# A hybrid decoder layer on one core: small products of a pair of heads gathered into fewer groups on TensorE

## The chip, the core and the metric

The kernel runs on one core of a Trainium2 chip. The metric is the device time of one execution in microseconds (us). A core has TensorE (matrix products, written PE in the profile), VectorE (DVE), ScalarE (ACT), GpSimd (POOL) and SyncE (SP, which here issues the transfers). Products write into PSUM, which is divided into banks; a bank here holds a tile of 128 x 512 in fp32.

## The reference, cut to what matters

One layer with width 2048 and 512 tokens. A single input projection feeds two token mixers; their outputs are projected up, merged by gates, projected out, and a per-layer embedding and two norms follow.

```
h = rmsnorm(x);  z = h @ w_in          # columns: r,k,v,g (RWKV), q,k,v,g (FoX), gates
# RWKV-7, 16 heads of 64, one step per token:
s_kk = S @ kk_t
S = S * w_t - outer(s_kk, kk_t * a_t) + outer(v_t, k_t);   y_t = S @ r_t
y = group_norm(y) + (sum r*k*r_k) * v;   y_rw = y * silu(g)
# FoX, 16 heads of 64, causal blocks of 128 queries:
logits = q k^T / 8 + (c_q - c_k);  probs = softmax(causal(logits));  o = probs @ v
y_fox = o * silu(g)
merged = sigmoid(gate_rw) * (y_rw @ w_up_rwkv) + sigmoid(gate_fox) * (y_fox @ w_up_fox)
x = x + merged @ w_out
x = x + (p @ ple_proj) * sigmoid(rmsnorm(x) @ ple_gate_w);   out = rmsnorm(x)
```

## The kernel before, in words

**Weight products.** Activations lie transposed, a tile being 128 columns of the width by all 512 tokens. Each fp32 weight is split into a high part (`hi`, a cast on ScalarE, L154) and a rest (`lo`, a subtraction on VectorE, L155), and so are the activations (`xh`, `xl`). Per tile of 128 rows of a weight three products of 128 x 512 are summed: xh with hi, xl with hi, xh with lo. `main` (L788) is a generator that issues them step by step: for each of eight pairs of heads p the eight projections rw_k, rw_v, rw_r, rw_g, fx_k, fx_q, fx_v, fx_g (128 columns each, 48 products each), then gates (`gate`), upward projections (`up`), output (`wo`) and embedding (`pp`, `pg`).

**Small products.** What the two mixers compute is small fp32 work. `rw_mixer` (L413) and `fox_mixer` (L685) are coroutines, one of each per pair. `Tensor` (L54) adds up an estimated time of TensorE, in ns; `Streams` (L73) resumes a coroutine when the number of ns that its last `yield` named have passed. It then issues a few products, which so stand between the weight products. TensorE's order is thus set by the yields. The other engines' order, and with it that of their waits, is set by a scheduler that looks at readiness in its own estimate; only the `keep` operations hold their places. An engine works its queue strictly in order.

**RWKV of a pair.** Tokens go in eight chunks of 64, q = 0, 1 being halves of four chunks. After transposing the inputs (`at`, `bt`, `kt`, L484 to L503), the products of a chunk give the matrices inside it (`gb`, L526; `gk`, L541). A part of gb, `lt`, goes through HBM and comes back spread over partitions as `lr` (L537 to L540). With it VectorE inverts 32 x 32 triangles by 60 operations in a row on `tp` and `nn` (L571 to L579). The inverses leave by transfer into `mdr` and come back twice, as `mt` and as the diagonal blocks; both land in the buffer `bd`. Two transposes on VectorE (L588) make from it the `x` that the products x3 and x4 (L590 to L602) combine; x3's result is copied by ScalarE at L595. Then `u` (L606), `tr` and `py` (L618 to L634), the state chunk by chunk (`st`, L636 to L643), group norm with a power on GpSimd (L656 to L667), and the output.

**Attention of a pair.** Two heads, four blocks of 128 queries each. Per block: decays (GpSimd, L721); logits `lg` on TensorE; a reduction on VectorE that masks and takes the maximum (`nm`, L732); exponential (ScalarE, L734), reciprocal (VectorE, L735), scaling (ScalarE, L736); transposes `pT` on TensorE (L755); a copy `pt` (ScalarE, L758); values `po` on TensorE (L769). Once per pair the values are transposed too (`fvt`, L689, copied at L693).

**Banks.** main has two banks for weight products, "A" two (gb, gk, u, x, transposes of RWKV), "F" one (lg, pT, fvt), "Y" two (py), "O" one (po). A group that needs a bank waits until its last reader is through. `pt` has two buffers.

**Names.** A name in the order has the pair behind it (x3 of pair 6 is x36); attention's have head and block (pT12_0: head 12, block 0), and a number that only tells one use of a buffer from another.

Of the kernel before, what the change touches and what calls it, by code (L numbers as in the profile page):

```python
# [15 lines left out]
F32 = mybir.dt.float32  # L16
# [7 lines left out]
P = 128  # L24
T = 512
# [82 lines left out]
def build(tc, a, out, dbg=None):  # L108
# [3 lines left out]
    v, s, g, dma = nc.vector, nc.scalar, nc.gpsimd, nc.sync  # L112
    keep = tc.keep_in_program_order
    pe = Tensor(nc.tensor)
# [118 lines left out]
    for h in range(2):  # L233
        hs = slice(64 * h, 64 * h + 64)
# [44 lines left out]
    psx = mix.enter_context(tc.tile_pool(name="psx", bufs=1, space=PSUM))  # L279
# [11 lines left out]
    small = {}  # L291
# [105 lines left out]
    def b2(name):  # L397
        return big.tile([P, T], F32, tag="b2", bufs=B2, name=name)

    def b4(shape, name):  # L400
        return big.tile(shape, F32, tag="b4", bufs=7, name=name)

    def psa(shape, name):
        return psx.tile(shape, F32, tag="A", bufs=2, name=name)

    def c3(t):
        return t.rearrange("p (c t) -> p c t", t=64)

    def need(z, *names):
        while any(n not in z for n in names):  # L410
            yield 450

    def rw_mixer(p, z):  # L413
# [12 lines left out]
        for h in range(2):  # L426
            cs = slice(P * h, P * h + P)
            v.tensor_tensor(lul[half(h), cs], lur[half(h), cs], luh[half(h), cs].bitcast(F32), op=ALU.subtract)
        yield 4700
        for h, (dst, hc) in enumerate(((sig, p), (aa, 8 + p))):  # L430
            cs = slice(P * h, P * h + P)
            ps = psa([P, T], f"lo{h}_{p}")
# [19 lines left out]
        kr, kr2, kp = b2(f"kr{p}"), b2(f"kr2{p}"), b2(f"kp{p}")  # L452
# [7 lines left out]
        v.tensor_tensor(k, k, aa, op=ALU.mult)  # L460
        v.tensor_tensor(kp, k, ip, op=ALU.mult)
        bdb, bdk = small["bd", 0], small["bd", 1]
        for h in range(2):
            s.copy(bdb[half(h), :, half(h)], c3(kr)[half(h)])
        for h in range(2):
# [16 lines left out]
        av, ba, ka = (b4([P, NC, P], f"{n}{p}") for n in ("av", "ba", "ka"))  # L482

        def token_major(name, pieces):  # L484
            ps = psa([P, 4, 2, 64], f"{name}{p}")
            for j in range(4):
                pe.transpose(ps[:, j], pieces(j), ident)
            return ps

        def by_heads(dst, ps):  # L490
            for h in range(2):
                for par in range(2):
                    s.copy(dst[half(h), par:NC:2], ps[half(par), :, h])

        by_heads(av[:, :, 0:64], token_major("at", lambda j: ar[:, 0, 2 * j : 2 * j + 2].rearrange("p c t -> p (c t)")))
        yield 5000 if p == 0 else 2700
        ps = token_major("bt", lambda j: kr[:, j * P : (j + 1) * P])
        for h in range(2):
            for par in range(2):
                v.tensor_tensor(ba[half(h), par:NC:2, 64:128], ps[half(par), :, h],  # L500
                                n2[half(h), par:NC:2].to_broadcast([64, 4, 64]), op=ALU.mult)
        yield 4000 if p == 0 else 2400
        by_heads(ka[:, :, 64:128], token_major("kt", lambda j: kp[:, j * P : (j + 1) * P]))  # L503
        yield from need(z, "v")
        vv = z["v"]
        yield 3500
# [15 lines left out]
        lt = c3(b2(f"lt{p}"))  # L522
        lak, mt = small["bd", 2], small["bd", 3]
        smb = lambda cs, n: sm[:, cs].unsqueeze(1).to_broadcast([P, 4, 64])[n]
        for q in range(2):
            cs = slice(4 * q, 4 * q + 4)  # L526
            ps = psa([P, 4, P], f"gb{p}_{q}")
            for j in range(4):
                pe.matmul(ps[:, j], bdb[:, 4 * q + j], ar[:, :, 4 * q + j], start=True, stop=True)
            v.tensor_tensor(lt[:, cs], ps[:, :, 0:64], c3(ms)[:, cs], op=ALU.mult)  # L530
            v.tensor_tensor(ba[:, cs, 0:64], ps[:, :, 64:128], c3(mi)[:, cs], op=ALU.mult)
            yield 900

        ldr = dr.tile([32, 32, 32], F32, tag="ldr", name=f"ldr{p}")
        mdr = dr.tile([32, 32, 32], F32, tag="mdr", name=f"mdr{p}")
# [2 lines left out]
            dma.dma_start(ldr[i : i + 8].rearrange("c i t -> i c t"), lt[bs, :, 32 * b : 32 * b + 32])  # L538
        lr = b4([P, 32, 32], f"lr{p}")
        dma.dma_start(lr, ldr.unsqueeze(0).to_broadcast([4, 32, 32, 32]).rearrange("g q i t -> g q (i t)"))  # L540
        for q in range(2):  # L541
            cs = slice(4 * q, 4 * q + 4)
            ps = psa([P, 4, P], f"gk{p}_{q}")
            for j in range(4):
                pe.matmul(ps[:, j], bdk[:, 4 * q + j], ar[:, :, 4 * q + j], start=True, stop=True)
            for h in range(2):
                v.tensor_tensor(lak[half(h), cs, half(h)], ps[half(h), :, 0:64],
                                smb(slice(0, 64), half(h)), op=ALU.mult)
            v.tensor_tensor(ka[:, cs, 0:64], ps[:, :, 64:128], smb(slice(64, 128), slice(0, P)), op=ALU.mult)
            yield 900  # L550
        ps = psa([P, T], f"bo{p}")
        pe.matmul(ps, bonesr, rh, start=True, stop=False)
        pe.matmul(ps, bonesr, rl, start=False, stop=True)
        bv = b2(f"bv{p}")
        v.tensor_tensor(bv, ps, vv, op=ALU.mult)
        yield 500

        ps = psa([P, NC, 64], f"rv{p}")
        for c in range(NC):
# [6 lines left out]
        v.scalar_tensor_tensor(sg, sg, 1.0, z["g"], op0=ALU.add, op1=ALU.mult)  # L566
        nn = big.tile([P, 8, 32], F32, tag="nn", bufs=1, name=f"nn{p}")
        tp = big.tile([P, 8, 32], F32, tag="tp", bufs=1, name=f"tp{p}")
        yield 4450

        keep(v.tensor_tensor(tp, ninit[:, :, 0:1].to_broadcast([P, 8, 32]), lr[:, 0:1, :].to_broadcast([P, 8, 32]), op=ALU.mult))  # L571
        v.tensor_tensor(nn, ninit, tp, op=ALU.add)
# [17 lines left out]
        ps = psa([P, NC, 32], f"x3{p}")  # L590
# [6 lines left out]
        ps = psa([P, NC, 32], f"x4{p}")  # L597
# [5 lines left out]
        yield 2000  # L603

        bua, buv = bdb, bdk
        for q in range(2):  # L606
            cs = slice(4 * q, 4 * q + 4)
            ps = psa([P, 4, P], f"u{p}_{q}")
            for j in range(4):
                pe.matmul(ps[:, j], mt[:, 4 * q + j], av[:, 4 * q + j], start=True, stop=True)  # L610
            for dst, at in ((bua, slice(0, 64)), (buv, slice(64, 128))):
                for h in range(2):
                    s.copy(dst[half(h), cs, half(h)], ps[half(h), :, at])
            yield 2000

        tr = b4([P, NC, P], f"tr{p}")
        py = []
        for q in range(2):  # L618
            j0 = 1 - q
            cs = slice(4 * q + j0, 4 * q + 4)  # L620
            ps = psa([P, 4, P], f"tr{p}_{q}")
            for j in range(j0, 4):
                pe.matmul(ps[:, j], bua[:, 4 * q + j], ba[:, 4 * q + j], start=True, stop=True)
            v.tensor_tensor(tr[:, cs, 0:64], ps[:, j0:, 0:64], ar[:, 1, cs], op=ALU.add)
            v.tensor_tensor(tr[:, cs, 64:128], ps[:, j0:, 64:128],
                            stack.unsqueeze(1).to_broadcast([P, 4 - j0, 64]), op=ALU.add)
            yield 300
            one = psx.tile([P, 4, P], F32, tag="Y", bufs=2, name=f"py{p}_{q}")
            for j in range(4):
                c = 4 * q + j  # L630
                pe.matmul(one[:, j], ba[:, c], buv[:, c], start=j == 0, stop=False, skip=True)
                pe.matmul(one[:, j], ka[:, c], vbd[:, c], start=False, stop=c == 0, skip=True)
            py.append(one)
            yield 900  # L634

        for c in range(1, NC):  # L636
            st = small["st", c % 2]
# [31 lines left out]
        ps = psa([P, T], f"yt{p}")  # L669
# [15 lines left out]
    def fox_mixer(p, z):  # L685
        vt = f2(f"fvt{p}").rearrange("p (j d) -> p j d", d=P)
        done = []

        def token_major():  # L689
            ps = psf([P, 4, P], f"fvt{p}")  # L690
            for j in range(4):
                pe.transpose(ps[:, j], z["v"][:, j * P : (j + 1) * P], ident)
            s.copy(vt, ps)  # L693
            done.append(1)

        yield from need(z, "k", "q")
        q, k = z["q"], z["k"]
# [3 lines left out]
        for h in range(2):  # L701
            hs, ho = slice(64 * h, 64 * h + 64), slice(64 - 64 * h, 128 - 64 * h)
# [6 lines left out]
        o = f2(f"fo{p}")  # L709
        blocks = [(h, i) for h in range(2) for i in range(4)]  # L710
        cb, dds, pos = {}, {}, {}
# [13 lines left out]
        def weights(h, i):  # L725
# [9 lines left out]
            v.reciprocal(nm[:, 1:2], nm[:, 1:2])  # L735
            s.activation(dd[:, :n], dd[:, :n], AF.Copy, scale=nm[:, 1:2])  # L736


        fetch(0)
        yield 4000  # L740
# [1 line left out]
        yield 1500  # L742
        weights(0, 0)
        for b, (h, i) in enumerate(blocks):
            hs, n = slice(64 * h, 64 * h + 64), (i + 1) * P
            if (h, i) == (0, 3):
                fetch(1)
                yield 4000
            if b < 7:
                decays(*blocks[b + 1])  # L750
                yield 1500
                weights(*blocks[b + 1])
            yield 2600 if b < 7 else 5500
            ps = psf([P, 4, P], f"pT{2 * p + h}_{i}")
            for j in range(i + 1):  # L755
                pe.transpose(ps[:, j], dds[h, i][:, j * P : (j + 1) * P], ident)
            pt = big.tile([P, 4, P], F32, tag="pt", bufs=2, name=f"pt{2 * p + h}_{i}")
            s.copy(pt[:, 0 : i + 1], ps[:, 0 : i + 1])  # L758
            yield 2600
            if not done:  # L760
                yield from need(z, "v")
                yield 700
                token_major()
                yield 1500
            if i == 0:

                pos[h] = psx.tile([P, T], F32, tag="O", bufs=1, name=f"po{p}_{h}")
            for j in range(i + 1):
                pe.matmul(pos[h][:, i * P : n], vt[:, j], pt[:, j], start=(j == 0), stop=(j == i))  # L769
            if i == 3:  # L770
                s.copy(o[hs], pos[h][hs])
        yield from need(z, "g")
        sg = f2(f"fsg{p}")
        s.activation(sg, z["g"], AF.Tanh)
# [335 lines left out]
```

## Time and profile before

| | |
|---|---|
| three runs | 1919.41, 1920.49, 1921.46 us; median 1920.49 |
| profiled execution | 1920.65 us, span 1918.9 us |
| TensorE, products | busy 1875.8 us, 98% of the span, 9704 |
| TensorE, weight loads | 1568.4 us, 82% |
| VectorE | 1052.1 us, 55%, 2239 instructions |
| ScalarE | 850.2 us, 44%, 1606 |
| GpSimd | 178.6 us, 9%, 296 |
| HBM | 106 GB/s over the span |

Busy time is the sum of the drawn lengths of an engine's instructions, as a share of the span, which reaches from the first to the last instruction on the core. TensorE's products overlap in the drawing: one is drawn longer than the distance to the next, so 98% busy leaves open how much waiting lies within. Idle time of VectorE and ScalarE costs nothing by itself; what counts is where TensorE waits for them.

### The profile page before, as it was taken

To read this page: it belongs to the slowest core of one execution; us is meant where nothing else is said; L and a number is where in the kernel's file an instruction comes from. 1 tells how busy PE (TensorE), PEld (TensorE's weight loads), DVE (VectorE), ACT (ScalarE), POOL (GpSimd) and SP (SyncE) were. 2 spreads that over 40 slices of the span, in tenths; PEclk is the share of its full clock that TensorE was granted. 3 is DMA by queue.
4 is the path that set the end of the run, shared out by engine and by line. 5 is a ranking of instruction groups with operands and counts; after the bars stand their busy time and mean duration, and the time that the engine had idled before them with its cause. 6 is when DMAs were issued, how large, how long until landed. Compare 5 with 4: busy or idle time off the path is not lost.

```text
span 1918.9 us, 26128 instructions
## 1 busy us (share of the span) xinstructions
PE 1875.8 (98%) x9704; PEld 1568.4 (82%) x9704; DVE 1052.1 (55%) x2239; ACT 850.2 (44%) x1606; POOL 178.6 (9%) x296
## 2 busy tenths in 40 slices
PE   7989999999999999999999999999999999999997
PEld 5878888888888888888887888888888888878887
DVE  8775667757577575775754433343333533434445
ACT  6536456373563735636346322232222433334333
POOL 6201001010010100101000000000000001101112
PEclk9999999999999999999999999999999999999998
DMA  5231322322223232232323533242322244453324
GB/s 169 93 94 65 97 85 81 108 71 97 88 82 107 69 96 88 85 105 65 99 82 111 181 114 106 93 143 99 99 96 93 98 142 152 154 199 99 99 95 158
DMA packets 87391, 204.31 MB, mean 106 GB/s; under 512 B 24784, under 2 KB 31184, under 8 KB 87264
## 3 DMA queue, kind: packets, MB, share of 16 engines
q1 hardware_dynamic: 85888, 201.39, 32.3%
q8 instruction: 76, 1.25, 0.3%
q10 hardware_dynamic: 1376, 1.25, 0.2%
q14 instruction: 51, 0.42, 0.1%
HBM read 186.06 MB, written 16.55 MB: 106 GB/s over the span
## 4 chain that ended last, share of the span: by engine, by line
PE 56%; ACT 1%; DVE 1%; issue 0%; POOL 0%; DVEq 0%; POOLq 0%; ACTq 0%
PE gate L62 18%; PE pg L62 9%; PE up L62 9%; PE wo L62 9%; PE rw_g L62 1%; PE fx_g L62 1%; PE pp L62 1%; PE fx_v L62 1%; PE fx_q L62 1%; PE fx_k L62 1%; PE rw_k L62 1%; PE py L62 1%; PE po L62 0%; PE pT L69 0%; PE rw_r L62 0%
## 5 line engine op out<-in xcount | busy, mean ns | idle before, releaser
L154 ACT CAST hi<-raw 128x512 fp32r<-128x512 f32 x596 | 368.4, 621 | 783.9 <-PE gate L62 208.1
L155 DVE TENSOR_TENSOR lo<-raw,hi 128x512 fp32r<-128x512 f32 x596 | 415.7, 699 | 452.5 <-ACT hi L154 449.3
L62 PE MATMUL gate<-xh,hi 128*128 128x512 f32 x512 | 201.0, 393 | 0.0
L62 PE MATMUL gate<-xh,lo 128*128 128x512 f32 x512 | 199.4, 389 | 0.0
L62 PE MATMUL gate<-xl,hi 128*128 128x512 f32 x512 | 199.3, 389 | 0.0
L62 PEld LDWEIGHTS gate<-xh,lo 128*128 128x128 f32 x512 | 96.1, 188 | 20.2
L62 PEld LDWEIGHTS gate<-xl,hi 128*128 128x128 f32 x512 | 96.2, 188 | 19.3
L62 PEld LDWEIGHTS gate<-xh,hi 128*128 128x128 f32 x512 | 96.1, 188 | 19.2
L62 PE MATMUL pg<-x2h,hi 128*128 128x512 f32 (+1 forms) x304 | 108.8, 358 | 0.5 <-ACT hi L154 0.5
L62 PE MATMUL pg<-x2h,lo 128*128 128x512 f32 (+1 forms) x304 | 108.2, 356 | 0.0
L62 PE MATMUL pg<-x2l,hi 128*128 128x512 f32 (+1 forms) x304 | 108.1, 356 | 0.0
L721 POOL TENSOR_SCALAR dd<-cb,cq 128x128 f32<-128x128 f32 (+1 forms) x64 | 39.6, 620 | 564.9 <-PE pT L69 530.3
L906 POOL TENSOR_TENSOR acc<-acc,sq 128x512 f32<-128x512 f32 x15 | 19.4, 1296 | 654.3 <-ACT sq L905 654.3
L577 DVE TENSOR_TENSOR tp<-nn,lr 128x240 f32<-128x240 f32 (+14 forms) x240 | 69.0, 287 | 6.4
L579 DVE TENSOR_TENSOR nn<-nn,tp 128x240 f32<-128x240 f32 (+14 forms) x240 | 68.8, 287 | 6.5
L62 PEld LDWEIGHTS pg<-x2h,hi 128*128 128x128 f32 x304 | 57.4, 189 | 9.2 <-ACT hi L154 0.9
L62 PEld LDWEIGHTS pg<-x2h,lo 128*128 128x128 f32 x304 | 57.4, 189 | 8.6 <-DVE lo L155 0.4
L62 PEld LDWEIGHTS pg<-x2l,hi 128*128 128x128 f32 x304 | 57.5, 189 | 8.3 <-issue 0.2
L734 ACT ACTIVATE dd<-dd,nm 128x128 f32<-128x128 f32 (+1 forms) x64 | 35.9, 561 | 45.5 <-DVE nm L732 45.3
L62 PE MATMUL rw_v<-xh,hi 128*128 128x512 f32 x128 | 53.5, 418 | 2.0 <-DVE zt L286 2.0
L62 PE MATMUL fx_g<-xh,hi 128*128 128x512 f32 x128 | 53.5, 418 | 0.0
L62 PE MATMUL rw_g<-xh,hi 128*128 128x512 f32 x128 | 53.3, 417 | 0.0
(540 smaller groups left out, 4426.0 us busy)
## 6 DMA issues: line engine op xcount, KB each, us to landing
raw<-in_w_mix SPq DMA_DIRECT2D x126, 512.0 KB, 3.7
raw<-in_w_gate SPq DMA_DIRECT2D x64, 512.0 KB, 3.9
raw<-in_w_pg SPq DMA_DIRECT2D x36, 512.0 KB, 3.7
raw<-in_w_out SPq DMA_DIRECT2D x32, 512.0 KB, 3.9
raw<-in_w_up_rw SPq DMA_DIRECT2D x16, 512.0 KB, 3.4
raw<-in_w_up_fox SPq DMA_DIRECT2D x16, 512.0 KB, 3.4
x<-in_xT SPq DMA_DIRECT2D x16, 256.0 KB, 5.0
cb<-cdr SPq DMA_DIRECT2D x16, 256.0 KB, 3.3
```

Source lines behind the costliest of these rows:

```text
L62: self.eng.matmul(out, lhsT, rhs, start=start, stop=stop, skip_group_check=skip)
L154: s.copy(hi[:, :w], src)
L155: v.tensor_tensor(lo[:, :w], src, hi[:, :w].bitcast(F32), op=ALU.subtract)
L577: v.tensor_tensor(tp[:, :, 0:m], nn[:, :, j : j + 1].to_broadcast([P, 8, m]), lr[:, j : j + 1, j + 1 : 32].to_broadcast([P, 8, m]), op=ALU ...
L579: v.tensor_tensor(nn[:, :, j + 1 : 32], nn[:, :, j + 1 : 32], tp[:, :, 0:m], op=ALU.add)
L721: g.tensor_scalar(dd[:, :n], cb[h][:, :n], -1.0, cq[:, i, hd : hd + 1], op0=ALU.mult, op1=ALU.add)
L734: s.activation(dd[:, :n], dd[:, :n], AF.Exp, scale=-1.0, bias=nm[:, 0:1], accum_out=nm[:, 1:2])
L906: g.tensor_tensor(acc, acc, sq, op=ALU.add)
```

## The change

- `gb`, `gk`, `u` and `tr` with `py`: the products of both halves are issued together, and only then the operations that read them. Before, a half's products were followed by its reads and a `yield`.
- `kt`'s transposes follow directly behind `bt`'s.
- `bo` is issued directly ahead of `rv`, with no yield between.
- Attention's `po` of a block is issued behind `pT` of the next block (`late`), the last one by itself at the end; the yields around it go.
- ScalarE's copies into the buffers `bdb` and `bdk` wait, in steps of 450 ns, until the previous pair's `py` is issued.
- The yields are set anew.

```diff
         bdb, bdk = small["bd", 0], small["bd", 1]
+        while p > 0 and ("py", p - 1) not in small:
+            yield 450
...
-        yield 5000 if p == 0 else 2700
+        yield 6000 if p == 0 else 3600
         ps = token_major("bt", lambda j: kr[:, j * P : (j + 1) * P])
+        pk = token_major("kt", lambda j: kp[:, j * P : (j + 1) * P])
...
-        yield 4000 if p == 0 else 2400
-        by_heads(ka[:, :, 64:128], token_major("kt", lambda j: kp[:, j * P : (j + 1) * P]))
+        by_heads(ka[:, :, 64:128], pk)
...
+        both = []
         for q in range(2):
-            cs = slice(4 * q, 4 * q + 4)
             ps = psa([P, 4, P], f"gb{p}_{q}")
             for j in range(4):
                 pe.matmul(ps[:, j], bdb[:, 4 * q + j], ar[:, :, 4 * q + j], start=True, stop=True)
+            both.append(ps)
+        for q, ps in enumerate(both):
+            cs = slice(4 * q, 4 * q + 4)
             v.tensor_tensor(lt[:, cs], ps[:, :, 0:64], c3(ms)[:, cs], op=ALU.mult)
             v.tensor_tensor(ba[:, cs, 0:64], ps[:, :, 64:128], c3(mi)[:, cs], op=ALU.mult)
-            yield 900
...
+        yield 3500                       # ahead of gk, which is treated like gb
...
-            yield 900                    # behind each half of gk
+        yield 5000                       # behind gk
         ps = psa([P, T], f"bo{p}")
...
-        yield 500                        # between bo and rv
...
-        yield 4450                       # ahead of the chain on tp and nn
+        yield 1200
...
-            yield 2000                   # behind each half of u
+        yield 4600                       # behind both
...
-            yield 300                    # between tr and py
...
-            yield 900                    # behind each half of py
+        yield 900
+        small["py", p] = True
...
+        def values(h, i, pt):
+            hs = slice(64 * h, 64 * h + 64)
+            if i == 0:
+                pos[h] = psx.tile([P, T], F32, tag="O", bufs=1, name=f"po{p}_{h}")
+            for j in range(i + 1):
+                pe.matmul(pos[h][:, i * P : (i + 1) * P], vt[:, j], pt[:, j], start=(j == 0), stop=(j == i))
+            if i == 3:
+                s.copy(o[hs], pos[h][hs])
+        late = []
...
             s.copy(pt[:, 0 : i + 1], ps[:, 0 : i + 1])
-            yield 2600
+            if late:
+                late.pop()()
+            late.append(lambda h=h, i=i, pt=pt: values(h, i, pt))
             if not done:
                 yield from need(z, "v")
                 yield 700
                 token_major()            # fvt
-                yield 1500
...
+        yield 2600
+        late.pop()()
```

**How the order moves on VectorE.** The place is pair 6 around the start of attention, while fx_g is computed. dd12_0 and nm12_0 are the decays and the norm of block 0 of head 12 (the reduction names both), dd12_1 those of block 1; x36 are the two transposes that wait for the transfers into bd3; lo are weight splits; the row of nn6 is the last of the chain. The order before:

```order
L579 TENSOR_TENSOR nn6_7980<-nn6_7980,tp6_7981 128x8
L155 TENSOR_TENSOR lo226_8255<-raw226_8252,hi226_8254 128x512
L825 TENSOR_TENSOR fzv6_8275<-fx6_v_8184,rb_111 128x512
L155 TENSOR_TENSOR lo227_8279<-raw226_8252,hi227_8278 128x512
L732 ISA dd12_0_8264,nm12_0_8285<-lg12_0_8286,dd12_0_8264 128x128
L732 ISA nm12_0_8285 128x1
L735 RECIPROCAL nm12_0_8285<-nm12_0_8285 128x1
L732 ISA dd12_1_8293,nm12_1_8304<-lg12_1_8305,dd12_1_8293 128x256
L732 ISA nm12_1_8304 128x1
L155 TENSOR_TENSOR lo228_8320<-raw228_8317,hi228_8319 128x512
L735 RECIPROCAL nm12_1_8304<-nm12_1_8304 128x1
L588 STREAM_TRANSPOSE x36_8172<-bd3_525 32x256 x2
```

And now, from the reduction of block 0 on:

```order
L742 ISA dd12_0_8264,nm12_0_8287<-lg12_0_8288,dd12_0_8264 128x128
L742 ISA nm12_0_8287 128x1
L595 STREAM_TRANSPOSE x36_8147<-bd3_525 32x256
L745 RECIPROCAL nm12_0_8287<-nm12_0_8287 128x1
L742 ISA dd12_1_8295,nm12_1_8306<-lg12_1_8307,dd12_1_8295 128x256
L742 ISA nm12_1_8306 128x1
L595 STREAM_TRANSPOSE x36_8147<-bd3_525 32x256
L155 TENSOR_TENSOR lo228_8320<-raw228_8317,hi228_8319 128x512
L745 RECIPROCAL nm12_1_8306<-nm12_1_8306 128x1
```

The two transposes have moved: one stands ahead of block 0's reciprocal and block 1's reduction, the other ahead of block 1's reciprocal, where both stood behind all of them.

On TensorE, at the same place, `fvt` now follows `pT` of block 0 after three weight products; before, eighteen stood between. The order now:

```order
L62 MATMUL fx6_g_8279<-xh6_263,lo225_8237 128x512
L69 MATMUL pT12_0_8332<-ident_71,dd12_0_8264 128x128
L62 MATMUL fx6_g_8279<-xh7_298,hi225_8236 128x512
L62 MATMUL fx6_g_8279<-xl7_299,hi225_8236 128x512
L62 MATMUL fx6_g_8279<-xh7_298,lo225_8237 128x512
L69 MATMUL fvt6_8339<-ident_71,fzv6_8277 128x128 x4
```

Both use the one "F" bank, and so the second comes after the copy that reads the first.

**How the order moves on ScalarE.** The place is pair 6 after fvt's copy. x36 are here the two copies of x3's result, dd12_2 the weights of block 2. Before:

```order
L693 COPY fvt6_7976<-fvt6_8364 128x512
L154 CAST hi231_8389<-raw230_8355 128x512
L595 COPY x36_8172<-x36_8396 32x256 x2
L734 ACTIVATE dd12_2_8378,nm12_2_8415<-dd12_2_8378,nm12_2_8415 128x384
L736 ACTIVATE dd12_2_8378<-dd12_2_8378,nm12_2_8415 128x384
```

Now:

```order
L703 COPY fvt6_7976<-fvt6_8339 128x512
L744 ACTIVATE dd12_2_8345,nm12_2_8360<-dd12_2_8345,nm12_2_8360 128x384
L154 CAST hi230_8395<-raw230_8393 128x512
L746 ACTIVATE dd12_2_8345<-dd12_2_8345,nm12_2_8360 128x384
L602 COPY x36_8147<-x36_8374 32x256 x2
L778 COPY pt12_1_8405<-pT12_1_8402 128x256
```

The copies of x have moved behind exponential, cast and scaling of block 2.

## Rows read from the trace of the kernel before

**Rows 1.** Chain of work that ended last, its longest piece: start, us, what
```profile
1049.22 54.41 PE gate L62 x240
```

**Rows 2.** TensorE's waits: product, what ended them, us in total, times, longest
```profile
PE lg L62 <- DVE nm L732: 5.8, 2, 5.1
PE pT L69 <- DVE nm L732: 5.6, 7, 0.8
PE py L62 <- DVE st L640: 2.5, 7, 0.7
PE gb L62 <- DVE ar L514: 1.2, 1, 1.2
PE po L62 <- ACT pt L758: 1.0, 1, 1.0
```

**Rows 3.** Timeline of TensorE: start, us, instruction, count, idle before it and releaser
```profile
518.42 0.38 PE L62 MATMUL py<-bd,ba 128*128 128x128 f32 x2
...
519.97 0.39 PE L62 MATMUL py<-bd,ka 128*128 128x128 f32 x2
...
805.50 1.05 PE L62 MATMUL gb<-ar,bd 128*128 128x128 f32 x8
806.31 0.48 PE L62 MATMUL rw_g<-xh,hi 128*128 128x512 f32 x1
806.62 0.40 PE L62 MATMUL rw_g<-xl,hi 128*128 128x512 f32 x1
```

**Rows 4.** Timeline of TensorE, pair 6, head 13, block 2
```profile
915.79 0.39 PE L62 MATMUL rw_r<-xh,lo 128*128 128x512 f32 x1
916.98 0.55 PE L69 MATMUL pT<-ident,dd 128*128 128x128 f32 x3 [0.80 <-DVE nm L732]
```

**Rows 5.** Timeline of VectorE at the same place
```profile
914.80 0.17 DVE L663 TENSOR_TENSOR nt<-rst 128x8 f32<-128x8 f32 x1 [1.77 <-POOL rst L662]
...
916.23 0.68 DVE L732 CUSTOM_DVE_ANT_0 dd<-lg,dd 128x512 f32<-128x512 f32 x1
```

**Rows 6.** Timeline of VectorE, pair 6, start of attention
```profile
851.92 0.18 DVE L579 TENSOR_TENSOR nn<-nn,tp 128x8 f32<-128x8 f32 x1
...
855.00 0.42 DVE L732 CUSTOM_DVE_ANT_0 dd<-lg,dd 128x256 f32<-128x256 f32 x1
...
856.01 0.69 DVE L155 TENSOR_TENSOR lo<-raw,hi 128x512 fp32r<-128x512 f32 x1 [0.58 <-ACT hi L154]
...
857.18 0.43 DVE L588 STREAM_TRANSPOSE x<-bd 32x256 f32<-32x256 f32 x1 [0.41 <-DMA bd<-mdr]
...
858.21 0.44 DVE L588 STREAM_TRANSPOSE x<-bd 32x256 f32<-32x256 f32 x1 [0.59 <-DMA bd<-mdr]
```

**Rows 7.** Timeline of SP's queue, pair 0
```profile
99.21 0.68 SPq L540 DMA_DIRECT2D lr<-ldr  x1
```

**Rows 8.** Timeline of VectorE, pair 0, the chain's start
```profile
108.93 0.43 DVE L571 TENSOR_TENSOR tp<-ninit,lr 128x256 f32<-128x256 f32 x1 [3.86 <-DMA lr<-ldr]
```

**Rows 9.** Timeline of TensorE, pair 6, start of attention
```profile
857.44 0.27 PE L69 MATMUL pT<-ident,dd 128*128 128x128 f32 x1
...
865.82 0.44 PE L62 MATMUL lg<-ks,qs 128*128 128x384 f32 x1
```

**Rows 10.** Timeline of ScalarE, pair 6, start of attention
```profile
856.81 0.51 ACT L736 ACTIVATE dd<-dd,nm 128x256 f32<-128x256 f32 x1 [0.33 <-DVE nm L735]
857.75 0.27 ACT L758 COPY pt<-pT 128x128 f32<-128x128 f32 x1 [0.43 <-PE pT L69]
...
865.94 0.75 ACT L595 COPY x<-x 32x256 f32<-32x256 f32 x2 [0.94 <-PE x L62]
867.18 0.61 ACT L734 ACTIVATE dd<-dd,nm 128x384 f32<-128x384 f32 x1 [0.49 <-DVE nm L732]
...
868.12 0.62 ACT L736 ACTIVATE dd<-dd,nm 128x384 f32<-128x384 f32 x1 [0.23 <-DVE nm L735]
```

**Rows 11.** Windows, pair 0: stretch, us; PE, PEld, DVE, ACT, POOL; PEclk, DMA, GB/s
```profile
132.80:138.00 5.20, 5.14 (x13) 4.18 (x14) 4.32 (x23) 2.52 (x7) 0.00 (x0) 0.50 0.31 101
```

More of the change, by code (lines that the diff above doesn't have):

```diff
@@ L540, in rw_mixer @@
         dma.dma_start(lr, ldr.unsqueeze(0).to_broadcast([4, 32, 32, 32]).rearrange("g q i t -> g q (i t)"))
+        yield 3500
+        both = []
         for q in range(2):
-            cs = slice(4 * q, 4 * q + 4)
             ps = psa([P, 4, P], f"gk{p}_{q}")
@@ L545, in rw_mixer @@
                 pe.matmul(ps[:, j], bdk[:, 4 * q + j], ar[:, :, 4 * q + j], start=True, stop=True)
+            both.append(ps)
+        for q, ps in enumerate(both):
+            cs = slice(4 * q, 4 * q + 4)
             for h in range(2):
@@ L605, in rw_mixer @@
         bua, buv = bdb, bdk
+        both = []
         for q in range(2):
-            cs = slice(4 * q, 4 * q + 4)
             ps = psa([P, 4, P], f"u{p}_{q}")
@@ L610, in rw_mixer @@
                 pe.matmul(ps[:, j], mt[:, 4 * q + j], av[:, 4 * q + j], start=True, stop=True)
+            both.append(ps)
+        for q, ps in enumerate(both):
+            cs = slice(4 * q, 4 * q + 4)
             for dst, at in ((bua, slice(0, 64)), (buv, slice(64, 128))):
@@ L744, in fox_mixer @@
         for b, (h, i) in enumerate(blocks):
-            hs, n = slice(64 * h, 64 * h + 64), (i + 1) * P
             if (h, i) == (0, 3):
@@ L763, in fox_mixer @@
                 token_major()
-                yield 1500
[L765 to L771, printed above, removed]
+        yield 2600
+        late.pop()()
         yield from need(z, "g")
```

## The prediction, made before the changed kernel ran

> **What bounds the kernel now.** I read the chain of waits first, to see which engine carries the end, then TensorE's waits, to see what there is to win, and then the timelines of one pair. In the chain the reader is to see runs of TensorE without a break: 240 products of the gates in 54.41 us, 0.227 us each [rows 1]. TensorE is the bound, and outside its own work only its waits can be won. The list of waits [rows 2] is short: 5.6 us where pT (the transposes of attention's weights) wait for VectorE, 2.5 us where py waits for the state, single waits of 1.2 us (gb) and 1.0 us (po), and one of 5.1 us at a logit product (lg) in pair 0. A wait costs 0.16 us more than its row says, since a product is drawn 0.39 us long and the next may start after 0.227. The trace is that of pairs of heads p = 0 to 7; I argue on pair 6, whose pattern repeats from pair 2 on.
>
> **What a group of small products costs.** The change is about groups of fp32 products between the weight products. Inside such a group a pass takes 0.111 us: py's 14 passes from 518.42 to 519.97 us [rows 3]. Eight passes of gb and the weight product behind them take 806.62 - 805.50 = 1.12 us, and 8 x 0.111 + 0.227 is 1.115 [rows 3]. So going into a group and out again costs next to nothing; what is left is that weight products behind a group follow each other at 0.23 instead of 0.227 for some steps. I take 0.03 us a group. Counted in the order of instructions there are 235 such groups before and 181 after, so the change does half of what its words say, since many small products stood together already. That is 54 x 0.03 = -1.6 us, with 0 at one end; at the other the weight product behind a group, which is drawn 0.31 long (806.31 to 806.62) and so 0.085 too long: -4.6 us.
>
> **What goes.** In pairs 1 to 7 pT of the second head's third block waits 0.80 us [rows 4]: it started 1.19 us after the product ahead of it, so 0.96 is lost. It waits because it shares the one "F" bank with the next block's logits, whose reduction on VectorE (L732) stands behind the group norm, and that waits 1.77 us for GpSimd's power [rows 5]. In the new order this reduction stands ahead of the group norm: -6.7 us for seven (0 at the other end, if ScalarE's work ahead of it now does the same). py's seven waits cost 2.5 + 7 x 0.16 = 3.6 us; they come from state copies in crowded queues, which are no less crowded after; I take half, -1.8 (0 to -3.6). Of gb's and po's single waits (2.2 + 0.3) half too: -1.2 (0 to -2.5).
>
> **What comes: VectorE stands still for a transfer, now ahead of the logits.** The chain of 60 small VectorE operations ends at 852.10 us in pair 6; two transposes (L588) wait for the two transfers behind it and start 5.08 and 6.11 us later [rows 6]. Before, both logit reductions and both reciprocals of blocks 0 and 1 stand ahead of them, so this standing still cost TensorE nothing. In the new order VectorE has: reduction 0, transpose, reciprocal 0, reduction 1, transpose, weight split, reciprocal 1. Nothing behind the first transpose runs before its transfer has landed.
>
> When does it land? The chain starts when the gate product has passed ScalarE and VectorE and when lr has landed. In the new order bo and rv stand behind the last product of rw_g, so the gate path is 2 x 0.227 + 16 x 0.111 = 2.2 us earlier against fx_k. lr can decide instead: in pair 0 its transfer was issued at 99.21 [rows 7] and VectorE stood idle for it until 108.93 [rows 8], and from gb to fx_k there are now 10.1 us of TensorE's work, not 11.5, counted in the two orders at 0.111 a pass and 0.227 a weight product. One weight split more (0.69, [rows 6]) lies inside the chain. So the chain ends between 0 and 2.2 - 0.7 = 1.5 us earlier against fx_g; I take 1.0, nearer to the gate path, since only pair 0 shows a wait for lr.
>
> In pair 6's clock, with the chain 1.0 earlier: first transpose from 856.18 (0.43), reciprocal 0 (some 0.2, an estimate by its single column), reduction 1 (0.42): done at 857.23, just in time for pT at 857.44 [rows 9]. Second transpose to 857.66; then weight split and reciprocal 1, which before took from 856.01 until ScalarE began to scale at 856.81 [rows 6, 10], 0.80: to 858.46. Then on ScalarE the scaling of block 1 (0.51) and only behind it the copy of pT (0.27) [rows 10]: 859.24. The next user of the "F" bank is fvt, which the change puts 3 weight products behind pT (18 before): due at 857.44 + 0.11 + 3 x 0.227 = 858.23. It comes 1.0 us late, 7 x 1.0 = +7.0 us. With the chain 1.5 earlier it is 0.5 a pair (+3.5), with the chain no earlier 2.0 (+14).
>
> **What else comes.** The two copies of x (0.75) now stand on ScalarE behind exponential and scaling of block 2. These end 868.74 - 865.82 = 2.92 us after their logits start [rows 9, 10]; a weight cast that now lies between adds 0.3, so the copies end 3.97 after. x4, the product that reads them, is due 0.35 (the logits) + 6 x 0.227 + 0.70 (x's products) + 3 x 0.227 + 4 x 0.111 = 3.53 after: 0.4 us late, +2.8 us for seven (0 to 5.6). kt needs the second "A" bank, which at held, so it waits for at's four copies, at the end of some 9 us in which ScalarE has no gap, in my count of its queue; with the smaller waits around it 0.3 a pair, +2.1 (0 to 5.6). The wait for the previous pair's py only delays ScalarE's copies into two buffers that py read anyway; behind it stand block 3's scaling and pT's copy, and I count it in this 0.3. In pair 0 gb comes earlier, the chain starts 4 us earlier, but the first logit reduction now stands one step before the chain's end instead of ten; I get 0.9 us more for its 5.1 us wait (-2 to +3). Attention's values cost nothing by being late: they read pt, of which there are two, and their output leaves after block 3 only.
>
> Both halves of a product at once fill both "A" banks, so the next user waits until both are read. Between gb and gk stand 9 weight products, 2.0 us, and the four operations that read gb are 128 x 256 each, 0.43 by one of that size [rows 8], 1.7 together; so here it costs nothing. The Trainium skill (Perfetto Trace Analysis, Matmuls) says that independent groups should rotate through the banks, so that one is read out while the next is computed; this speaks against the change. By it each of the pairs' doubled groups would show its read-out, by the row 0 for gb, gk and u, and only kt has it, in the 0.3 above.
>
> **Sum.** -1.6 - 6.7 - 1.8 - 1.2 + 7.0 + 2.8 + 2.1 + 0.9 = +1.5 us. The profiled execution took 1920.65 us (span 1918.9), 0.16 above the median shown, so 1922 us.
>
> **Rivals.**
> - Slower: the chain starts no earlier because lr's landing sets it, and fvt waits 2.0 us in each pair from 1 on. For it speaks pair 0, where VectorE waited 3.86 us for lr [rows 8]; against it, that no later pair shows such a wait. +7.0 on the sum: 1929 us. It decides from a first transpose some 4.6 us behind the start of fx_g on.
> - Slower by the clock: fvt's wait and the one before it fall close together, and the granted clock drops in each pair. In pair 0, behind the 5.1 us wait, it was 0.50 for the 5.2 us looked at [rows 11], which is 1.2 GHz; waits of 1 us left it at 1. With half of 5.2 us lost in seven pairs, +18: 1940 us. The Trainium skill (TensorE: Matmul & The Clock Gate, Why this matters for your kernels) warns of idle gaps between bursts of products; by that rule this case is real, though the trace shows it for the long wait alone.
> - Faster: the new waits shrink to fvt's 0.5 a pair, x's copies are in time, and what goes is gone: 3.5 (fvt) + 2.8 (x) + 1.4 (kt) = 7.7 us off the sum, 1914 us. For it speaks that pT's wait has one clear cause, which the new order removes.
> - The change does nothing by what it is meant for: a group costs nothing at all, and the sum is 1.6 higher, 1924 us.
>
> **Chances.** Forecast 0.30, no gain from groups 0.08 (both within 0.2%), lr 0.28, clock 0.08, faster 0.26. Within 0.2%, 3.8 us either way of the median, is what a measurement here can't tell from no change: faster 0.26, same 0.38, slower 0.36. Range 1911 to 1939, which takes in the faster rival with more of py's waits gone, and nearly the clock's; the forecast's own is 1917 to 1925.
>
> **What would show it.** VectorE: the first transpose ahead of the second reduction, waiting for bd, in each pair. TensorE: new waits at fvt (about 1 us) and at x4 (0.4), none at pT of the second head's third block. Wrong would be: no wait at fvt, pT waiting itself (the transfer later than I think), waits at tr or gk (banks), or weight products at less than 0.227 us behind groups.

## The result, and the profile after

The changed kernel takes 1941.59 us (median of 4 runs, 1938.63 to 1947.30) against 1920.97 for the kernel before (4 runs, 1919.41 to 1923.19): a ratio of 1.0111, 95% interval 1.0096 to 1.0125. It is 20.6 us slower; forecast were 1922, with a range of 1911 to 1939. The profiled execution took 1947.30 us (span 1945.6), the longest of the four, so its waits are read pair by pair below and not as a mean of all runs.

TensorE's waits after the change (engine, product, what ended them, us in total, times, longest), to be read beside [rows 2]:

```profile
PE pT L69 <- ACT dd L746: 8.4, 5, 2.2
PE fvt L69 <- ACT pt L778: 7.0, 7, 1.4
PE lg L62 <- DVE nm L742: 6.9, 3, 5.3
...
PE vt L69 <- DVE nt L674: 3.6, 6, 0.6
...
PE pcr L69 <- ACT ka L495: 1.6, 1, 1.6
...
PE vt L69 <- DVE var L671: 0.5, 1, 0.5
PE pT L69 <- DVE nm L742: 0.3, 1, 0.3
```

Everything that stood there before is gone but the lg wait of pair 0: pT behind the group norm, py, gb, po. In their place stand pT and fvt, the first transposes of a pair (fvt in pairs 1 to 7, pT in all of these but pair 2), and vt, a transpose of the next pair. Rows of the first 60 us and of the end of the kernel are left out, and three single waits (lo 0.7, po 0.3, lg 0.2).

VectorE in pair 6 at the start of attention, which answers to [rows 6] (start, us, instruction, idle before it and releaser):

```profile
876.85 0.28 DVE L742 CUSTOM_DVE_ANT_0 dd<-lg,dd 128x128 f32<-128x128 f32 x1
...
881.37 0.43 DVE L595 STREAM_TRANSPOSE x<-bd 32x256 f32<-32x256 f32 x1 [4.22 <-DMA bd<-mdr]
881.74 0.11 DVE L745 RECIPROCAL nm<-nm 128x1 f32<-128x1 f32 x1
881.78 0.39 DVE L742 CUSTOM_DVE_ANT_0 dd<-lg,dd 128x256 f32<-128x256 f32 x1
...
882.35 0.44 DVE L595 STREAM_TRANSPOSE x<-bd 32x256 f32<-32x256 f32 x1 [0.17 <-DMA bd<-mdr]
```

VectorE stands still for 4.22 us, with block 0's reciprocal and block 1's reduction queued behind the transpose. ScalarE, same place, waits for that reciprocal:

```profile
881.88 0.40 ACT L746 ACTIVATE dd<-dd,nm 128x128 f32<-128x128 f32 x1 [4.20 <-DVE nm L745]
...
884.04 0.25 ACT L778 COPY pt<-pT 128x128 f32<-128x128 f32 x1
```

And TensorE, which needs block 0's weights scaled for pT and the copy of pT made for fvt (beside [rows 9]):

```profile
882.34 0.33 PE L69 MATMUL pT<-ident,dd 128*128 128x128 f32 x1 [1.48 <-ACT dd L746]
...
884.34 0.66 PE L69 MATMUL fvt<-ident,fzv 128*128 128x128 f32 x4 [0.98 <-ACT pt L778]
```

In pair 6 fx_g starts at 875.45, so the first transpose stands 5.9 us behind the start of fx_g; it was 5.0 before, and I had counted on 4.0. In pairs 1 to 7 it stands at 4.8, 4.5, 5.9, 6.7, 7.6, 5.9 and 6.7.

The clock (windows view: stretch, us, PE, PEld, DVE, ACT, POOL, granted clock, DMA share, GB/s), around the two waits in pairs 3, 4, 5 and 6:

```profile
505.00:515.00 10.00, 7.22 (x27) 5.47 (x26) 3.56 (x10) 3.40 (x9) 1.20 (x2) 0.83 0.44 120
630.00:640.00 10.00, 7.04 (x21) 5.59 (x22) 3.41 (x11) 3.88 (x10) 1.40 (x2) 0.66 0.42 118
757.00:767.00 10.00, 8.06 (x54) 6.26 (x54) 3.47 (x12) 4.56 (x12) 1.40 (x2) 0.66 0.38 114
880.00:885.00 5.00, 2.55 (x13) 1.59 (x12) 2.18 (x8) 2.60 (x7) 1.41 (x2) 1.00 0.49 129
```

Where the two waits come to 2.8 us (pair 3), 3.1 (4) and 3.05 (5), the granted clock over the 10 us looked at is 0.83, 0.66 and 0.66; in pairs 6 and 7 (2.5 and 2.2 us) it stayed at full speed. The share that is missing of each 10 us is 1.7, 3.4 and 3.4 us, 8.5 together. That it takes both waits is not shown: in pair 4 the granted clock was 0.50 already from 632.9 to 633.1 us, behind pT's wait of 2.2 us and ahead of fvt's.

### The profile page after: what moved, and what is told of

Read it like the earlier page. It is cut to its first block, busy times and chain, and to the rows that moved or that the text cites. A ratio compares the mean times of both kernels' runs of the same rounds, so it can differ in the third digit from the quotient of the medians.

```text
span 1945.6 us, 26167 instructions
## 1 busy us (share of the span) xinstructions
PE 1888.0 (97%) x9704; PEld 1577.2 (81%) x9704; DVE 1049.9 (54%) x2239; ACT 846.2 (43%) x1604; POOL 182.8 (9%) x296
## 4 chain that ended last, share of the span: by engine, by line
PE 76%; DVE 10%; DMA 4%; ACT 4%; issue 1%; POOL 1%; SPq 0%; DVEq 0%; ACTq 0%
PE gate L62 18%; PE pg L62 9%; PE up L62 9%; PE wo L62 9%; PE rw_k L62 4%; PE rw_g L62 4%; PE fx_g L62 3%; PE fx_k L62 3%; DVE lo L155 2%; PE rw_r L62 2%; PE rw_v L62 2%; DVE nn L586 2%; PE py L62 2%; DVE tp L584 2%; PE fx_q L62 2%; DMA lr<-ldr 2%
## 5 line engine op out<-in xcount | busy, mean ns | idle before, releaser
L731 POOL TENSOR_SCALAR dd<-cb,cq 128x128 f32<-128x128 f32 (+1 forms) x64 | 40.2, 629 | 636.0 <-PE pT L69 522.2
L62 PE MATMUL fx_g<-xh,hi 128*128 128x512 f32 x128 | 58.1, 454 | 0.0
L62 PE MATMUL fx_g<-xl,hi 128*128 128x512 f32 x128 | 52.9, 413 | 0.0
```

What stands on the lines that cost most here:

```text
L62: self.eng.matmul(out, lhsT, rhs, start=start, stop=stop, skip_group_check=skip)
L731: g.tensor_scalar(dd[:, :n], cb[h][:, :n], -1.0, cq[:, i, hd : hd + 1], op0=ALU.mult, op1=ALU.add)
```

## The experiments

Theory A: VectorE standing still ahead of block 1's reduction is what costs, by the waits at pT and fvt and the clock behind them. Theory B: the doubled groups cost, by their banks. Theory C: attention's late values cost.

**e1.** The changed kernel, the transposes of x issued 4.5 us later.

```diff
-        yield 14500
+        yield 19000
         for h in range(2):
             keep(v.transpose(x3[lo(h)], mt[lo(h), :, lo(h)]))
-        yield 9500
+        yield 5000
```

> The changed kernel with one edit: the two transposes of x are issued 4.5 us (by TensorE's estimate) later, which puts them on VectorE behind the reductions and reciprocals of blocks 0 and 1 again; TensorE's order stays that of the changed kernel. Theory A (VectorE stands still for the transfer ahead of the logits, and TensorE waits at pT and fvt, with the clock falling behind the longer waits): those waits, 16 us in the profiled run, go, the clock stays up in pairs 1 to 7, and the time falls by 17 to 24 us to 1917 to 1925. Theory B (the doubled groups themselves cost, by banks that are read out late): waits lie spread over the RWKV products and the time stays over 1932. Theory C (attention's values one block late are what costs): over 1932 too, with the waits still at pT or po.

1918.54 us (10 runs; ratio to before 0.9988, 0.9979 to 0.9998). All of the loss is gone with this one move: theory A. The traces of the two kernels show how little was moved: from pair 1 on TensorE and ScalarE run the same instructions in the same order in both, and VectorE's order differs in the two transposes alone. VectorE in pair 6 now runs the reduction and the reciprocal ahead of the transposes, which still wait, to nobody's harm:

```profile
855.20 0.42 DVE L742 CUSTOM_DVE_ANT_0 dd<-lg,dd 128x256 f32<-128x256 f32 x1 [0.28 <-PE lg L62]
...
856.93 0.16 DVE L745 RECIPROCAL nm<-nm 128x1 f32<-128x1 f32 x1
857.45 0.43 DVE L595 STREAM_TRANSPOSE x<-bd 32x256 f32<-32x256 f32 x1 [0.37 <-DMA bd<-mdr]
```

No wait at pT of block 0 or fvt is left, and the clock stays at full speed from 145 us to the gates. Among what stays are waits that come from RWKV's new timetable (vt) and from kt beside bt (pcr):

```profile
PE vt L69 <- DVE nt L674: 3.6, 6, 0.6
...
PE pcr L69 <- ACT ka L495: 1.6, 1, 1.6
```

**e2.** The changed kernel, kt's transposes back at their old place.

```diff
-        yield 6000 if p == 0 else 3600
+        yield 5000 if p == 0 else 2700
         ps = token_major("bt", ...)
-        pk = token_major("kt", ...)
...
-        by_heads(ka[:, :, 64:128], pk)
+        yield 4000 if p == 0 else 2400
+        by_heads(ka[:, :, 64:128], token_major("kt", ...))
```

> The changed kernel with kt's transposes at their old place, 2.4 us (4 in pair 0) behind bt's, and the yields ahead of them as before. If kt beside bt is what makes pcr wait 1.59 us for ScalarE in pair 0 and drops the clock to half behind it: that wait goes, pair 0 is 4 us shorter, nothing else changes: 1936 to 1939. If pair 0's loss is chance of the first 90 us: 1940 to 1943.

1940.0 us (4 runs; 1.0100, 1.0080 to 1.0119): in time not to be told from the changed kernel, and inconclusive on pair 0. pcr's wait is gone, and so are vt's; but py waits again (4.5 us, 7 times), and a logit product of pair 0 waits 3.0 us. What one wait gives up another takes.

**e3.** The changed kernel with attention as before (the old loop with `po` in its own block); RWKV changed.

> The changed kernel with attention as before (values in their own block, old yields); only the RWKV part is changed. The transposes of x still stand ahead of block 1's reduction on VectorE. Theory A: pT of block 0 needs the bank that this reduction frees, so it still waits 1 to 2 us in most pairs, but fvt has 18 products ahead of it again and does not wait: 7 us and part of the clock's loss less, 1928 to 1935. Theory C: all of the loss goes, 1918 to 1923. Theory B: 1938 or more.

1959.8 us (4 runs; 1.0209, 1.0194 to 1.0225). No theory had this: RWKV's part alone is worse than the whole change. fvt does not wait, as A has it, and pT waits 0.2 to 1.0; what costs is po, which waits 23.3 us in 15 places, 3.10 in each of six pairs. ScalarE in pair 6, second head, in e3:

```profile
951.43 0.62 ACT L746 ACTIVATE dd<-dd,nm 128x384 f32<-128x384 f32 x1 [3.05 <-DVE nm L745]
951.95 1.50 ACT L495 COPY vst<-vt 64x256 f32<-64x256 f32 x4
953.47 1.26 ACT L513 COPY bd<-vst 64x512 f32<-64x512 f32 x2
954.75 0.37 ACT L767 COPY pt<-pT 128x256 f32<-128x256 f32 x1
```

And TensorE in e3, which waits for that last copy:

```profile
955.18 0.71 PE L62 MATMUL po<-pt,fvt 128*128 128x128 f32 x4 [3.10 <-ACT pt L767]
```

ScalarE waits 3.05 us for a reciprocal that stands behind the group norm on VectorE, and then has six copies of RWKV ahead of pt. Before, po had nothing like it to wait for; with the values one block late, po has a block's time to spare. So the two parts are not a sum: late values are what makes the RWKV part bearable.

**e4.** The kernel before with late values and attention's new yields only.

> The kernel before with attention's values one block late and its new yields; RWKV as before. The transposes of x stand on VectorE behind both reductions as before. Theory A: no wait at pT of block 0, 0 to 0.3 us at fvt, the old wait of 0.8 us at the second head's third block gone: 1913 to 1919. Theory C: 1930 or more. Theory B: about 1920, since no group of RWKV is doubled.

1909.26 us (4 runs; 0.9945, 0.9930 to 0.9960), below its range: 11 us faster than before, and the fastest kernel of this study. From pair 2 to the end of attention its list of waits holds nothing; ahead of that it has, among others:

```profile
PE lg L62 <- DVE nm L732: 5.4, 1, 5.4
...
PE gb L62 <- DVE nt L664: 1.3, 1, 1.3
PE gk L62 <- ACT yt L673: 0.9, 1, 0.9
PE py L62 <- DVE st L640: 0.5, 1, 0.5
```

All four lie in pairs 0 and 1. From pair 2 on a pair takes 117.87 us (fx_g from 374.02 to 845.50, four pairs), and mostly 119.2 before. The old waits account for the 1.3 us: 0.96 at pT and 0.45 at py, 1.41 together. There are more groups in it than before (33 a pair for 31, counted in the traces with every small product).

**e5 and e6.** The move of e1 the other way, alone: in the kernel before by 2.5 us, and in e4's by 3.5.

```diff
-        yield 14500
+        yield 12000                      # e6: 11000
         for h in range(2):
             keep(v.transpose(x3[lo(h)], mt[lo(h), :, lo(h)]))
-        yield 9500
+        yield 12000                      # e6: 13000
```

> The kernel before with one edit: the two transposes of x are issued 2.5 us earlier, which puts them on VectorE where the change puts them, ahead of block 1's reduction and reciprocal; nothing else is changed. If standing still for the transfer is the cause by itself: pT of block 0 waits 0.5 to 0.7 us in each pair from 1 on (the transposes start 5.0 us behind fx_g's start, then 0.4 and a reduction of 0.4, where pT is due at 5.3), fvt has 18 products of cover and does not wait: 5 us more, 1923 to 1927. If it needs the changed RWKV part too: 1919 to 1922.

> Attention's values late, RWKV as before (the kernel that took 1909.3), and the transposes of x 3.5 us earlier, so that they stand ahead of block 1's reduction. With fvt three products behind pT both are exposed: pT 0.6, fvt 1.4 us, twice 0.16 on top, 16 us in seven pairs, and some pairs with the clock down: 1924 to 1932. If early transposes cost the same with either spacing of fvt: 1913 to 1916.

e5: 1925.21 us (10 runs; 1.0022, 1.0013 to 1.0032), 4.3 more than before. e6: 1924.64 us (10 runs; 1.0021, 1.0012 to 1.0030), 15.4 more than e4's kernel. Both as theory A has it. Between e4 and e6 the traces differ in the place of the two transposes on VectorE and in nothing else of the order of TensorE, ScalarE and VectorE, so the 15 us are theirs. With the values late, fvt stands close behind pT and both are exposed; e6 in pair 6:

```profile
862.78 0.30 PE L69 MATMUL pT<-ident,dd 128*128 128x128 f32 x1 [0.47 <-DVE nm L732]
...
864.65 0.33 PE L69 MATMUL fvt<-ident,fzv 128*128 128x128 f32 x1 [0.87 <-ACT pt L769]
```

The four corners: transposes late 1920.9 (values as before) and 1909.3 (values late), transposes early 1925.2 and 1924.6. Early transposes eat the whole gain of the late values.

**e7 and e9.** What sets the transfer's landing? Both are the changed kernel with lr meant to be earlier. e7 cut a wrong yield, so that vt came 2 us earlier and gk 2 us later, with gb and lr where they were; e9 cut the one ahead of gb.

```diff
         v.tensor_tensor(rl, r, rh.bitcast(F32), op=ALU.subtract)
-        yield 3500                       # e9; e7 cut the one behind vv = z["v"]
+        yield 1500
...
         dma.dma_start(lr, ...)
-        yield 3500                       # e7 and e9
+        yield 5500
```

> The changed kernel with gb 2 us earlier (the yield ahead of it 1.5 us for 3.5, the one ahead of gk 5.5 for 3.5), so that lr is issued 2 us earlier; the transposes stay ahead of block 1's reduction. If lr's landing sets the chain's start (VectorE waits for it in 7 pairs, 2.5 us in the mean), the chain and the transposes come 1.5 to 2 us earlier, the waits at pT and fvt shrink by that, the clock stays up, and the time is 1922 to 1930. If the gate's path sets it: 1939 to 1943.

> The changed kernel with the yield directly ahead of gb cut from 3.5 to 1.5 us, and the one ahead of gk 5.5 for 3.5 (e7 cut the yield ahead of vt by mistake, and left gb and lr where they were). lr is issued 2 us earlier against fx_g. If lr's landing sets the chain's start, the chain starts 1.5 to 1.9 us earlier, limited then by the gate's path (VectorE was through with it 1.75 us before lr landed in pair 6), the first transpose comes that much earlier, pT's waits of 1.2 to 2.2 us nearly go and fvt's stay near 1: 1926 to 1932. If the gate's path sets it: no move of the first transpose, 1939 to 1943.

e7: 1959.59 us (4 runs; 1.0201, 1.0184 to 1.0217). It says nothing on lr, but something on vt: 2 us earlier it waits 2.7 us instead of 0.6, in every pair. e9: 1940.1 us (4 runs; 1.0100, 1.0085 to 1.0115), no gain. lr was issued only 1.05 us earlier, since gb now waits for VectorE:

```profile
PE pT L69 <- ACT dd L746: 5.7, 6, 1.9
PE gb L62 <- DVE ar L516: 4.8, 7, 0.8
```

In pairs 1, 3 and 4 the chain then started 30.6 to 30.8 us ahead of fx_g, as early as the gate's path lets it (VectorE is through with that at 30.7), in the others 28.2 to 29.9. So lr does set the start where it can be told, and pT's waits fell from 8.7 to 5.7 us; gb's new waits took the same.

**e8.** e4's kernel with pair 0's attention 6 us later (`yield 4000 if p else 10000` ahead of its first decays).

> Attention's values late, RWKV as before (1909.3), and pair 0's attention 6 us later. In pair 0 the second logits wait 5.4 us for a reduction that stands in VectorE's queue among the chain; now that reduction stands behind the chain's end, some 4 us later, while the logits come 6 us later. The wait falls to 2 to 3.5 us, the clock behind it may stay down: 1904 to 1908. If the reduction moves as far as the logits do: 1909.

1911.19 us (4 runs; 0.9952, 0.9935 to 0.9968): not better than e4's. The wait fell from 5.4 to 3.8 us, and 1.5 at py and 0.6 more at gb came instead.

**e10 and e11.** The price of a group by itself, in the kernel before.

```diff
             step(ps, (hi[:, k], lo[:, k]), xs[kt], kt == 0, kt == n - 1)
+            for i in range(1):                          # e10: one behind each step
+            for i in range(n if kt == n - 1 else 0):    # e11: all behind the last step
+                pe.matmul(dum[:, 0:P], ident, ident, start=True, stop=True)
```

> The kernel before with 384 more fp32 products of 128 x 128 (identity by identity into a bank that nothing reads) in the second gates and upward products, one behind each three weight products: 384 groups of one. Against e11 the difference is the price of 352 ways into a group and out. At 0.03 us each, 10.6 us longer than e11; at the upper end of 0.085, 30 us; if a group costs nothing, within 2 us of it. The 384 products themselves cost 43 us at 0.111.

> The same 384 products in 32 groups, 16 behind each gate product and 8 behind each upward product. 1920.5 + 43 + 32 x 0.03 = 1964 us, and less than e10 by the price of 352 groups.

2011.96 us (4 runs) and 2007.88 us (4 runs). The products cost twice what I expected (87 us for 384, 0.227 each): a timeline draws a product of this size as two passes, and 0.111 us is the price of one. The difference is the answer: 4.1 us for 352 groups, 0.012 us each.

## Why the prediction was wrong

The step that failed is the one that asks when the transfer lands: "the chain ends between 0 and 2.2 - 0.7 = 1.5 us earlier against fx_g; I take 1.0", with the transfer behind the chain carried over at its old length, without a reason. That VectorE would stand still there, ahead of block 1's reduction, and that fvt would be late by it, was right, and e1, e5 and e6 show that it decides. But the first transpose came at 4.5 to 7.6 us behind fx_g's start, 6.0 in the mean of pairs 1 to 7, instead of 4.0, and in most pairs later than in the case that I had taken for the worst (5.0). In the prediction's sum fvt is late by this time less 3.0 us; with the measured times that gives 21 us in seven pairs where 7.0 were forecast, and TensorE lost 17.8 there, at pT and fvt together. So the mechanism held, and the size of the landing did not. Three things made it so; of the 1.9 us in pair 6 the first two make 0.7 and the third 1.2, and of the mean of 2.0 us over seven pairs 1.1 and 0.9:

- lr sets the chain's start. VectorE waits for it in 7 of 8 pairs, 17.6 us in all; before it did in pair 0 alone [rows 8]. The changed kernel's chain that ended last has the transfer in it (start, us, what):

```profile
461.75 10.20 DMA lr<-ldr
...
711.44 10.50 DMA lr<-ldr
836.30 10.17 DMA lr<-ldr
```

  Before, lr was issued 40.2 us ahead of fx_g and was there when the gate's path ended, 28.7 us ahead. After, the gate's path ends 30.7 us ahead, but lr is issued only 39.15 ahead. I had earlier gates in the sum, and later lr only as a rival (0.28). My own figures would have told: with 1.4 us less work between gb and fx_k lr is issued 38.8 us ahead, with 9.7 us from there to its use, as in pair 0 [rows 7, 8], it is there 29.1 us ahead, and the gate's path was forecast to end 30.9 ahead. In pair 6 the chain started 28.95 ahead.
- The chain is 0.5 us longer (28.6 for 28.1 in pair 6), by the weight split in it, of which I had counted 0.7.
- The transfer behind the chain takes longer. SP's queue in pair 6, in the changed kernel:

```profile
874.18 0.33 SPq L146 DMA_DIRECT2D raw<-in_w_mix  x1
875.12 0.55 SPq L587 DMA_DIRECT2D mdr<-nn  x1
879.51 1.81 SPq L589 DMA_DIRECT2D bd<-mdr  x4
```

The same place in the kernel before:

```profile
850.04 0.33 SPq L146 DMA_DIRECT2D raw<-in_w_mix  x1
852.12 0.53 SPq L580 DMA_DIRECT2D mdr<-nn  x1
855.42 1.81 SPq L582 DMA_DIRECT2D bd<-mdr  x4
```

  4.39 us from mdr's issue to that of the transfers that wait for it, instead of 3.30, with a weight transfer of 512 KB issued 0.94 us ahead of it instead of 2.08. The traces of all 13 kernels go the same way in pairs 1 to 7: with the weights 2.1 us ahead it took 3.3 to 3.5 us in 51 of 58 cases and 3.9 to 4.3 in the others, with the weights 0.9 us ahead 3.8 to 5.1 in all of 32. That the weights are the reason was not tried by moving them, so it stays open.

So pT, which I had "just in time", waited too, and around the two waits the clock fell in three pairs. What released pT was block 0's scaling on ScalarE (0.40 us, behind the reciprocal), which I had left out beside reduction 1; in pair 6 it ended 0.1 us later than that reduction. Both slower rivals came true in part, and at once, though I had each by itself, the clock with 0.08. Term by term (profiled execution, 0.16 us added to each wait):

| term | forecast, us | measured, us |
|---|---|---|
| groups | -1.6 | -0.6 (54 x 0.012, e10 and e11; -0.4 by the count below) |
| pT behind the group norm | -6.7 | -6.7, gone |
| py | -1.8 | -3.6, gone in all pairs |
| gb and po | -1.2 | -2.5, gone |
| fvt | +7.0 | +8.1 (7.0 + 7 x 0.16) |
| pT of block 0 | 0 | +9.7 (8.7 + 6 x 0.16) |
| x's copies at x4 | +2.8 | 0 |
| kt and small waits | +2.1 | +5.2 (vt, 4.1 + 7 x 0.16) |
| pcr in pair 0 | 0 | +1.8, and 3.4 by the clock around it |
| lg in pair 0, and new ones of 0.8 and 0.7 in pairs 5 and 7, for 0.7 in pair 1 before | +0.9 | +1.2 |
| clock in pairs 3 to 5 | 0 | +8.5 |

The sum is +24.5, beside 26.7 between the two profiled executions; 1.6 us of what is left is one wait of TensorE for GpSimd at 37 us (2.1 for 0.5). Between the medians it is 20.6. The clock goes far to account for the difference: the mean granted clock of the profiled execution was 0.988, that of the other three 0.991 to 0.992, and 0.003 of 1940 us is about 6 us, where the profiled execution was 5.2 to 8.7 us longer than they. So of the 12 us that the clock took in the profiled execution some 6 are left in the others, by this estimate. x's copies were just in time: in pair 6 the second ended at 889.98 and x4 started at 890.00.

The table also shows where I erred by place: kt costs nothing in the pairs; the group that pays for RWKV's new timetable is vt, whose input waits its turn on VectorE behind the group norm. In pair 0 kt beside bt fills both "A" banks, and pcr waits 1.59 us until ScalarE has read kt; with kt apart (e2) that wait is gone. The Trainium skill (Perfetto Trace Analysis, Matmuls) asks for groups to rotate through the banks so that one's read-out overlaps the next; here the trace agrees, with that 1.59 us, once where it could bite. Around it the granted clock was 0.66 in this execution:

```profile
82.00:92.00 10.00, 8.41 (x34) 6.52 (x33) 3.84 (x8) 3.10 (x8) 0.94 (x4) 0.66 0.27 82
```

In e1, with the same wait, it was at full speed:

```profile
82.00:92.00 10.00, 8.59 (x49) 7.36 (x50) 4.70 (x9) 6.41 (x14) 1.82 (x4) 1.00 0.25 84
```

On the clock the Trainium skill (TensorE: Matmul & The Clock Gate, Why this matters for your kernels) warns of idle gaps between bursts of products; the trace agrees in pairs 3 to 5, though no single wait there is longer than 2.2 us and the warning is of longer gaps, and it shows in pairs 6 and 7 that waits of nearly the same length can pass without it.

As for the change's aim: 54 groups fewer give back 0.6 us. Counted in the traces with every small product, logits too, there are 266 groups before and 234 after (31 and 27 a pair), which makes it 0.4. What was to be won lay in the waits, and of its two halves only the late values win them (e4); RWKV's part, without the transposes' harm, is e1 against e4: 1918.5 to 1909.3, 9 us worse, by vt (5.2), pcr (1.8) and a lower clock (0.993 in the mean of the profiled execution for 0.995, about 4 us by estimate); the other, smaller differences were not taken apart.

## What to carry to other kernels

An instruction that waits for a transfer holds everything behind it in its engine's queue, so look at what stands behind it and not at how long it waits: the same two transposes cost nothing behind the reductions and 15 us ahead of them. When several paths meet at a start (here the gate and lr), a change that shortens the one that decided brings out the next, and the next has to be priced before the gain is booked. And price the thing that a change sets out to save by itself first: 0.012 us a group would have told that nothing much was to be had there.

## What the runs showed of the hardware

- A way into a group of fp32 products and out again costs 0.012 us (e10 and e11). I had read 0.03 from one such group, where the rounding of the rows is as large as the price.
- An fp32 product of 128 x 128 x 128 is drawn as two passes, 0.111 us apart, and each of 384 of them made the run 0.227 us longer (e11 against before).
- lr, which reads 512 KB out of a 128 KB block in HBM (four times over, 32 partitions each), lands 9.0 to 10.5 us behind its issue in the changed kernel, and 8.6 to 11.4 in all traces, where VectorE waited for it; a weight load of the same size is listed at 3.7 on the page of before.
- A transfer of 128 KB into HBM (mdr) was through 3.3 us behind its issue in most cases when a weight transfer of 512 KB had been issued 2.1 us ahead of it, and 3.8 to 5.1 us when 0.9 us ahead (13 traces); the reason is open.
- At waits of 2.2 to 3.1 us in two pieces the granted clock fell in some pairs and not in others: in the changed kernel in pairs 3 to 5 and not in 6 and 7, in e2 in pair 4 (2.2 us) and not in pair 1 (2.5). At a wait of 1.59 us in pair 0 (pcr) it fell in three traces of five, and at waits of 5.1 to 5.4 us there in all nine that have one.
